# Products of zeros on TensorE inside each norm, between the transposes of two blocks of tokens and behind them

## The chip, the cores and the metric

The kernel runs on one core of one Trainium2 chip. The metric is the device time of one execution in microseconds (us), as the median of the runs. TensorE has two clock levels, 1.2 and 2.4 GHz; the profile shows the granted level of each stretch as a share (0.50 or 1.00). Engine names in the rows are the profile's: PE is TensorE's matmul, PEld its weight load, DVE VectorE, ACT ScalarE, POOL GpSimd, SP the queue that issues transfers.

## What the reference computes

Two blocks in a row on 256 tokens of 1024 features, all in float32. The first has two layers; in each, tokens `x` and a context `ctx` of 256 tokens are normalised, projected, run through a convolution and a two-way recurrent scan, projected back, normalised again and passed through a gated feed-forward layer (FFN):

```
ux = modulate(rmsnorm(x, norm1_g[l]), sh1, sc1) @ w_in[l]
...
x = x + gt1 * (mix_x @ w_out[l])
x = x + gt2 * swiglu(modulate(rmsnorm(x, norm2_g[l]), sh2, sc2), ffn_wg[l], ffn_wu[l], ffn_wd[l])
```

The context takes the same path in layer 0; in layer 1 only its scan states are needed. The second block has two layers of FFN, mixer and FFN, with a layer norm behind each:

```
x = layer_norm(ALPHA * x + 0.5 * swiglu_2(x, ffn1_w13[l], ffn1_w2[l]), ln_g[l, 0], ln_b[l, 0])
x = layer_norm(ALPHA * x + m, ln_g[l, 1], ln_b[l, 1])
x = layer_norm(ALPHA * x + 0.5 * swiglu_2(x, ffn2_w13[l], ffn2_w2[l]), ln_g[l, 2], ln_b[l, 2])
```

## The kernel before

All large products are made of three products of fp32r halves (high by high, high by low, low by high). Weights stream from HBM in tiles of 512 KB (`raw`); `wsplit` makes the high half on ACT (`wh`) and the low half on DVE (`wl`). Tokens stand in two blocks of 128, `b` = 0 and 1, one token to a partition, where the norms are computed: per block the statistics, then the scaled block `yb[b]`. The products need features on partitions, so `feature_major` transposes both blocks: eight transposes of 128x128 for each block on PE into four PSUM tiles (`acc`), where each tile holds two of the eight feature groups `f`, both blocks of each. Then ACT, DVE and POOL evacuate in an order written out by hand (`EVAC`): for each `f` a scaling out of PSUM ("e", over both blocks at once, lines 452 to 458), the high half ("h", line 460) and the low half ("l", line 462). The products that follow walk over `f`. In several norms (`PINS`, and all of the second part of the program) the splits of the third to sixth weight tile behind a norm are held back until the evacuation has ended (`hold`).

The path with `acc=True` is taken eleven times; the text numbers these norms in order of time. The first five are in the first part of the program (`self.tags is TAGS1`): the first before the FFN of the context, the second before its projection of layer 1, the third before the FFN of `x`, the fourth before the projection of `x` in layer 1, the fifth before its FFN. In the second part (`TAGS2`) the sixth is the closing norm of the first block, and the seventh to eleventh are the layer norms (`ln`) in front of mixers (seventh, tenth) and FFNs (eighth, ninth, eleventh). The first six are RMS norms: `rms_blocks` takes the sums of squares of both blocks first (line 416), then both square roots (384), then scales both blocks (423, 425). A layer norm does one block after the other (`ln_norm`, 406).

The order of instructions on each engine is set by a scheduler that runs when the program is built; `issue_after` fixes that one instruction stands behind another on its engine. PE executes its products in that order. `gate_row` builds a gate with eight small products (`tDb`, DVE line 519, PE, ACT copy 521) for the step behind the FFN. PSUM tiles `ps` and `pb` have two buffers each.

A tile of zeros, `zer`, is there already: in `chain` one product of zeros clears a bank ahead of products that accumulate into it.

Of the kernel before, what the change touches and what calls it, by code (L numbers as in the profile page):

```python
# [14 lines left out]
P = 128  # L15
D = 1024
NF = 8
T = 256
# [13 lines left out]
NFIRST = 2  # L32

NLATE = 3

NLAST = 2, 4

# [221 lines left out]
class Prog:  # L259
# [168 lines left out]
    def feature_major(self, yb, scale, bias, perm=False, new=None, acc=True):  # L428

        nc = self.nc  # L430
        new = new or self.S
        hs = [new([P, 4, T], F32R) for _ in range(2)]
        ls = [new([P, 4, T], F32R) for _ in range(2)]

        pt = [self.pacc(i) if acc else self.ps(lane="b") for i in range(4)]
        pt = [t.rearrange("p (j b t) -> p j b t", j=2, b=2) for t in pt]
        for f, b in [(f, b) for b in range(2) for f in range(NF)] if acc else [(f, b) for f in range(NF) for b in range(2)]:
            nc.tensor.transpose(pt[f // 2][:, f % 2, b, :], yb[b][:, f * P : f * P + P], self.cst("ident"))  # L438

        last, ts = {}, {}  # L440
        for e, op, f in (EVAC if acc else EVAC1):
            hi, lo = hs[f // 4][:, f % 4, :], ls[f // 4][:, f % 4, :]
            eng = {"A": nc.scalar, "D": nc.vector, "P": nc.gpsimd}[e]
            with self.tc.issue_after(last[e].ins) if e in last and acc else contextlib.nullcontext():
                if op == "e":
                    ts[f] = t = self.T1([P, T])
                    src, dst = pt[f // 2][:, f % 2].rearrange("p b t -> p (b t)"), t
                    if perm:
                        src = src.rearrange("p (r c) -> p r c", c=64)
                        dst = t.rearrange("p (c r) -> p r c", r=4)  # L450
                    if e == "A" and bias is None:
                        i = nc.scalar.activation(dst, src, AF.Copy, scale=scale(f))
                    elif e == "A":
                        i = nc.scalar.activation(dst, src, AF.Identity, bias=bias(f), scale=scale(f))
                    elif bias is None:
                        i = nc.vector.tensor_scalar(dst, src, scale(f), None, ALU.mult)
                    else:
                        i = nc.vector.tensor_scalar(dst, src, scale(f), bias(f), ALU.mult, ALU.add)
                elif op == "h":
                    i = nc.scalar.copy(hi, ts[f])  # L460
                else:
                    i = eng.tensor_sub(lo, ts[f], hi.bitcast(F32))
            last[e] = i
        la, ld = last["A"], last["D"]
        self.npin += 1
        if self.tags is TAGS2 or self.npin in PINS:
            self.hold, self.since = (la.ins, ld.ins), 0
        return [(hs[f // 4][:, f % 4, :], ls[f // 4][:, f % 4, :]) for f in range(NF)]

    def pacc(self, i):  # L470
        return self.t(self.pa, [P, 512], f"acc{i // 2}{i % 2}")
# [603 lines left out]
    def chain(self, g, AR, GR, KB, uv, r0, Q, pct, st, emit, yall, ends, banks=None):  # L1075

        nc = self.nc
        hd = [(p, d, h) for p in range(2) for d in range(2) for h in range(2)]
        AR, GR, KB = (x[2 * g : 2 * g + 2] for x in (AR, GR, KB))

        def ps(n):
            shape = (P, 2, 2, CH)
            return self.ps(shape) if banks is None else self.t(self.pa if n < 2 else self.pp, shape, banks[n])

        for i in range(4):
            jj = (i, 7 - i)
            sl = slice(i, 8 - i, 7 - 2 * i)
            if st is not None:
                p1 = ps(0)
                for p, d, h in hd:  # L1090
                    q = slice(h * 64, h * 64 + 64)
                    self.mm(p1[q, p, d, :], AR[p][q, d, jj[d] % 4, 0, :], st[q, p, d, :])
                rs = self.T1([P, 2, 2, CH])
                nc.vector.tensor_add(rs, p1, r0[:, :, sl, :])
                rr = lambda q, p, d: rs[q, p, d, :]
            else:
                rr = lambda q, p, d: r0[q, p, jj[d], :]
            pu = [ps(1), ps(0)]
            for p, d, h in hd:
                q = slice(h * 64, h * 64 + 64)  # L1100
                self.mm(pu[h][64:128, p, d, :], Q[d][q, (2 * g + p) * 4 + jj[d] % 4, :], rr(q, p, d))
            nc.scalar.mul(uv[0][64:128, :, sl, :], pu[0][64:128], -1.0)
            nc.vector.tensor_scalar(uv[1][64:128, :, sl, :], pu[1][64:128], -1.0, None, ALU.mult)
            pn = ps(1)
            for p, d, h in hd:
                q = slice(h * 64, h * 64 + 64)
                self.mm(pn[q, p, d, :], KB[p][:, jj[d], q], uv[h][:, p, jj[d], :])
            sn = self.t(self.pool, [P, 2, 2, CH], "st", bufs=5)
            pcb = pct[:, 2 * g : 2 * g + 2, sl].unsqueeze(3).broadcast_to([P, 2, 2, CH])
            if st is not None:  # L1110
                nc.vector.tensor_add(sn, pn, st)
                nc.vector.tensor_mul(sn, sn, pcb)
            else:
                nc.vector.tensor_mul(sn, pn, pcb)
            if emit:
                py = ps(2)
                kd = lambda d: d if i < 2 else 1 - d
                half = lambda h: slice(h * 64, h * 64 + 64)
                if st is not None:

                    self.mm(py.rearrange("p a b t -> p (a b t)"), self.zer[:, 0:P], self.zer, True, False)
                    for p, d, h in hd:
                        q = half(h)
                        self.mm(py[q, p, kd(d), :], st[q, p, d, :], AR[p][q, d, jj[d] % 4, 1, :], False, False)
                for n, (p, d, h) in enumerate(hd):
                    self.mm(py[half(h), p, kd(d), :], uv[h][:, p, jj[d], :], GR[p][:, h, jj[d], :], st is None,
                            st is None or n >= 6)
                lo = min(i, 3 - i)
                ysl = yall[:, 2 * g : 2 * g + 2, :].rearrange("p a (c t) -> p a c t", t=CH)[:, :, lo : 4 - lo : 3 - 2 * lo, :]
                if i < 2:  # L1130
                    nc.scalar.copy(ysl, py)
                else:
                    nc.vector.tensor_add(ysl, py, ysl)
            st = sn
            if i == 3:
                ends.append(st)
            yield
# [28 lines left out]
    def affine(self, x, y, g, b=None):  # L1166


        nc = self.nc
        for _ in range(NLATE):  # L1170
            yield
# [404 lines left out]
TAGS2 = {  # L1576
    ("S", "r"): ("S", 18), ("T1", "r"): ("T1", 10), ("T2", "r"): ("T2", 10), ("tD", "r"): ("tD", 2),
    ("tiny", "r"): ("tn", 8),
}


def body(tc, ap):
    k = Prog(tc, ap)
    with (
# [7 lines left out]
        mk = lambda pool, shape, name, dt=F32: pool.tile(shape, dt, name=name)  # L1592
# [2 lines left out]
        k.const = mk(pc, [P, NCONST], "const")  # L1595
        k.lb = [mk(pc, [P, 4], f"lb{l}") for l in range(2)]
        k.omlb = [mk(pc, [P, 4], f"omlb{l}") for l in range(2)]
        with (
            tc.tile_pool(name="p1", bufs=1) as p1,
            tc.tile_pool(name="pd", bufs=1, space=bass.MemoryType.DRAM) as pd,  # L1600
        ):
            k.pool, k.tags = p1, TAGS1
            k.csil = mk(p1, [P, 8, 32], "csil")
            k.zer = mk(p1, [1, T], "zer", mybir.dt.bfloat16)
            k.mod = [mk(p1, [P, 6, 8, 2], f"mod{l}") for l in range(2)]
            k.omka = [mk(p1, [P, 4], f"omka{l}") for l in range(2)]
            k.keep = [mk(pd, [P, D], f"keep{b}") for b in range(2)]
            k.first()
# [30 lines left out]
```

## Time and profile before

| | us |
|---|---|
| median of 3 runs | 2779.92 |
| lowest and highest run | 2776.57, 2785.88 |
| the profiled execution, its own time | 2783.58 |
| span of its instructions | 2781.8 |
| PE busy in the span | 2632.1 (95%) |
| ACT, DVE, POOL busy | 1327.3, 1716.4, 670.2 |

The profiled execution lies 3.66 above the median, and 1.8 of its time lies outside the span. A busy PE is not PE at its peak, since the ends of products are modelled and overlap. Times in rows count from the start of the span. `a<-b` is the tile written and the tiles read; `L438` is line 438; a bracket at a row's end gives the idle time ahead of it on its engine and what ended it.

### The profile page before, as it was taken

The page shows a single profiled execution, that of the slowest core. Times are in us where ns is not written, and L with a number is a line of the kernel's source. Part 1 is how long each engine was busy: PE and PEld are TensorE (multiplying, and loading weights), DVE is VectorE, ACT ScalarE, POOL GpSimd, SP SyncE. Part 2 cuts the span into 40 slices and gives each one's busy share as a digit, 9 for nine tenths or more (in the row PEclk, how much of TensorE's full clock was granted, in tenths as well). Part 3 has the DMA queues.
Part 4 walks back from the last instruction along what each step waited for, and adds up shares of the span by engine and source line. Part 5 has one row for each costly group of instructions (what it writes and reads, how often), then busy time and mean ns, then how long its engine had stood idle before and what let it go on. Part 6 is the DMA issues. An engine that isn't in the chain of part 4 may idle for free.

```text
span 2781.8 us, 53780 instructions
## 1 busy us (share of the span) xinstructions
PE 2632.1 (95%) x22398; PEld 2291.3 (82%) x22398; DVE 1716.4 (62%) x2703; ACT 1327.3 (48%) x2015; POOL 670.2 (24%) x669
## 2 busy tenths in 40 slices
PE   7889989999889998899899899999999999999998
PEld 4866867888678896866699899889899898889897
DVE  3885778645577555984555655666655655755655
ACT  5523654434565346433544544654544544644543
POOL 0388999920130001384200000010000000100000
PEclk9989989999899999979899999999999999999999
DMA  7345425334323354234355555524555555425653
GB/s 250 109 145 175 147 84 180 132 130 157 117 77 116 136 182 144 95 137 153 117 187 185 194 183 188 193 87 156 182 187 185 182 188 174 166 83 182 205 184 120
DMA packets 118768, 430.71 MB, mean 155 GB/s; under 512 B 13174, under 2 KB 13686, under 8 KB 118524
## 3 DMA queue, kind: packets, MB, share of 16 engines
q1 hardware_dynamic: 118524, 427.28, 45.2%
q8 instruction: 175, 2.87, 0.4%
q14 instruction: 69, 0.57, 0.1%
HBM read 425.13 MB, written 2.10 MB: 154 GB/s over the span
## 4 chain that ended last, share of the span: by engine, by line
PE 78%; DVE 11%; ACT 4%; POOL 3%; issue 2%; DMA 2%; SPq 0%; ACTq 0%; DVEq 0%; POOLq 0%
PE pb L333 33%; PE acc L333 25%; PE ps L333 19%; DVE wl L342 3%; DVE T1c L726 1%; POOL tap L732 1%; DVE S L964 1%; DVE T L962 1%; DMA raw<-in_ada 1%; DVE x L621 1%; ACT wh L341 1%; POOL x L733 1%; PE acc L438 1%; DMA raw<-in_wr 0%; DVE T2b L620 0%
## 5 line engine op out<-in xcount | busy, mean ns | idle before, releaser
L342 DVE TENSOR_TENSOR wl<-raw,wh 128x1024 fp32r<-128x1024 f32 (+1 forms) x654 | 811.9, 1245 | 622.2 <-ACT wh L341 391.7
L341 ACT CAST wh<-raw 128x1024 fp32r<-128x1024 f32 (+1 forms) x654 | 681.9, 1046 | 892.3 <-PE pb L333 345.8
L333 PE MATMUL pb<-xf,wh 128*128 128x256 f32 (+1 forms) x2560 | 486.4, 289 | 12.6 <-ACT T1b L585 4.1
L333 PE MATMUL pb<-S,wh 128*128 128x256 f32 x2560 | 492.0, 289 | 4.8 <-DVE S L631 1.8
L333 PEld LDWEIGHTS pb<-xf,wh 128*128 128x128 f32 (+1 forms) x2560 | 409.8, 194 | 26.7 <-DVE T1b L588 6.6
L333 PEld LDWEIGHTS pb<-S,wh 128*128 128x128 f32 x2560 | 408.5, 192 | 22.4 <-issue 11.8
L333 PE MATMUL ps<-S,wh 128*128 128x256 f32 x2048 | 390.4, 287 | 0.6 <-ACT S L460 0.5
L333 PE MATMUL pb<-xf,wl 128*128 128x256 f32 (+1 forms) x1280 | 371.2, 291 | 8.7 <-DVE wl L342 8.7
L365 POOL TENSOR_TENSOR wl<-raw,wh 128x1024 fp32r<-128x1024 f32 x22 | 54.9, 2504 | 1340.4 <-ACT wh L364 826.9
L333 PE MATMUL pb<-S,wl 128*128 128x256 f32 x1280 | 367.4, 287 | 2.0 <-DVE wl L342 2.0
L333 PEld LDWEIGHTS ps<-S,wh 128*128 128x128 f32 x2048 | 326.8, 192 | 9.0 <-issue 3.4
L333 PE MATMUL ps<-S,wl 128*128 128x256 f32 x1024 | 293.4, 286 | 0.6 <-DVE wl L342 0.6
L333 PEld LDWEIGHTS pb<-xf,wl 128*128 128x128 f32 (+1 forms) x1280 | 248.1, 194 | 16.7 <-DVE wl L342 11.5
L333 PEld LDWEIGHTS pb<-S,wl 128*128 128x128 f32 x1280 | 245.4, 192 | 6.6 <-issue 3.0
L333 PE MATMUL acc<-wh,T 128*128 128x512 f32 x704 | 206.3, 393 | 0.0
L333 PEld LDWEIGHTS ps<-S,wl 128*128 128x128 f32 x1024 | 196.7, 192 | 2.8 <-issue 1.4
L333 PE MATMUL acc<-wh,T1b 128*128 128x512 f32 x528 | 157.5, 396 | 3.5 <-ACT T1b L341 3.5
L732 POOL TENSOR_SCALAR tap<-z,cols 128x255 f32<-128x255 f32 (+14 forms) x120 | 149.2, 1252 | 0.0
L333 PEld LDWEIGHTS acc<-wh,T 128*128 128x128 f32 x704 | 126.9, 189 | 23.6
L732 POOL TENSOR_SCALAR tap<-x,cols 128x246 f32<-128x246 f32 (+6 forms) x104 | 111.4, 1079 | 46.1 <-DVE x L671 46.0
L733 POOL TENSOR_TENSOR x<-x,tap 128x247 f32<-128x247 f32 (+8 forms) x132 | 106.8, 809 | 34.4 <-ACT tap L730 28.0
L733 POOL TENSOR_TENSOR z<-z,tap 128x255 f32<-128x255 f32 (+14 forms) x120 | 112.8, 940 | 3.9
(445 smaller groups left out, 3968.7 us busy)
## 6 DMA issues: line engine op xcount, KB each, us to landing
raw<-in_fu SPq DMA_DIRECT2D x132, 512.0 KB, 3.2
raw<-in_ada SPq DMA_DIRECT2D x96, 512.0 KB, 4.3
raw<-in_pu SPq DMA_DIRECT2D x88, 512.0 KB, 4.2
raw<-in_qu SPq DMA_DIRECT2D x88, 512.0 KB, 3.7
raw<-in_fd SPq DMA_DIRECT2D x66, 512.0 KB, 3.2
raw<-in_wr SPq DMA_DIRECT2D x51, 512.0 KB, 3.6
raw<-in_pd SPq DMA_DIRECT2D x44, 512.0 KB, 4.1
raw<-in_qd SPq DMA_DIRECT2D x44, 512.0 KB, 3.8
```

Source lines behind the costliest of these rows:

```text
L333: return self.nc.tensor.matmul(out, lhsT, rhs, start=start, stop=stop, **kw)
L341: self.nc.scalar.copy(hi, src)
L342: self.nc.vector.tensor_sub(lo, src, hi.bitcast(F32))
L365: self.nc.gpsimd.tensor_sub(lo, r, hi.bitcast(F32))
L438: nc.tensor.transpose(pt[f // 2][:, f % 2, b, :], yb[b][:, f * P : f * P + P], self.cst("ident"))
L621: nc.vector.tensor_add(x[b][:, s], x[b][:, s], t)
L726: nc.vector.scalar_tensor_tensor(av[:, d], z[:, f, s], w(j), av[:, d], ALU.mult, ALU.add)
L732: nc.gpsimd.tensor_scalar(t[:, d], z[:, f, s], w(j), None, ALU.mult)
L733: nc.gpsimd.tensor_add(zc[f][:, d], zc[f][:, d], t[:, d])
L962: nc.vector.tensor_mul(tv, tj[:, k + 1 : 32, k : k + 1].broadcast_to([P, m, k + 1]), X[:, k : k + 1, 0 : k + 1].broadcast_to([P, m, k + 1]))
L964: nc.vector.tensor_sub(X[:, k + 1 : 32, 0 : k + 1], X[:, k + 1 : 32, 0 : k + 1], tv)
```

## The change

`feature_major` with `acc=True` chains the transposes: all eight of block 0, then `NZERO` products of zeros (128x128 by 128x256, bfloat16), all eight of block 1, then `NZEND` = 6 products of zeros. `NZERO` is 32 in the first part of the program and 14 in the second. Each such group writes a `ps` or `pb` tile that nobody reads. The tile `zer` grows from one partition to 128 and lives through the whole program; the one product in `chain` reads its first partition, as before.

```diff
+NZERO, NZEND = (32, 14), 6
...
+        last = None
         for f, b in [(f, b) for b in range(2) for f in range(NF)] if acc else [(f, b) for f in range(NF) for b in range(2)]:
-            nc.tensor.transpose(pt[f // 2][:, f % 2, b, :], yb[b][:, f * P : f * P + P], self.cst("ident"))
+            with self.tc.issue_after(last.ins) if last else contextlib.nullcontext():
+                i = nc.tensor.transpose(pt[f // 2][:, f % 2, b, :], yb[b][:, f * P : f * P + P], self.cst("ident"))
+            if acc and f == NF - 1:
+                last = self.zeros(i, (NZERO[self.tags is TAGS2], NZEND)[b])
...
+    def zeros(self, after, n):
+
+        pz = self.ps()
+        for _ in range(n):
+            with self.tc.issue_after(after.ins):
+                after = self.mm(pz[:, 0:T], self.zer[:, 0:P], self.zer)
+        return after
...
-                    self.mm(py.rearrange("p a b t -> p (a b t)"), self.zer[:, 0:P], self.zer, True, False)
+                    self.mm(py.rearrange("p a b t -> p (a b t)"), self.zer[0:1, 0:P], self.zer[0:1, 0:T], True, False)
...
+        k.zer = mk(pc, [P, T], "zer", mybir.dt.bfloat16)
...
-            k.zer = mk(p1, [1, T], "zer", mybir.dt.bfloat16)
```

PE's order around the fifth norm, before the change (`Sb_15174` is block 0, `Sb_15175` block 1, `x2` two transposes):

```order
L333 MATMUL acc_2600_15017<-wh_15134,xf_14950 128x512
L438 MATMUL acc_2643_15202<-const,Sb_15174 128x128 x2
L438 MATMUL acc_2644_15203<-const,Sb_15174 128x128 x2
L438 MATMUL acc_2643_15202<-const,Sb_15175 128x128 x2
L438 MATMUL acc_2644_15203<-const,Sb_15175 128x128 x2
L438 MATMUL acc_2645_15204<-const,Sb_15174 128x128 x2
L438 MATMUL acc_2646_15205<-const,Sb_15174 128x128 x2
L438 MATMUL acc_2645_15204<-const,Sb_15175 128x128 x2
L438 MATMUL acc_2646_15205<-const,Sb_15175 128x128 x2
L333 MATMUL pb_15299<-xf_15198,wh_15289 128x256
```

The same place now (lines are three to fifteen higher; `Sb_15334` is block 0, `Sb_15335` block 1; the pair of rows with `zer` stands 32 times at the first "..." and six times at the second):

```order
L336 MATMUL acc_2608_15177<-wh_15294,xf_15110 128x512
L443 MATMUL acc_2651_15362<-const,Sb_15334 128x128 x2
L443 MATMUL acc_2654_15365<-const,Sb_15334 128x128 x2
L336 LDWEIGHTS zer
L336 MATMUL pb_15374<-zer 128x256
...
L443 MATMUL acc_2651_15362<-const,Sb_15335 128x128 x2
L443 MATMUL acc_2654_15365<-const,Sb_15335 128x128 x2
L336 MATMUL pb_15415<-zer 128x256
...
L336 MATMUL pb_15455<-tDb_15456,const 128x128
L336 MATMUL pb_15469<-tDb_15470,const 128x128
L336 MATMUL pb_15499<-xf_15358,wh_15489 128x256
```

Before, four feature groups of each block came first and the rest behind; now the first transpose of block 1 stands behind all of block 0 and 32 products of zeros. Five products of the gate row (`tDb`), which stood ahead of the norm, now stand between the norm and the first product of the FFN. The same is so in the first and third norm; on DVE the eight `tDb` operations stand among the operations of the evacuation there.

PE's order around the seventh norm, a layer norm, before:

```order
L438 MATMUL acc_3292_19220<-const,S_19198 128x128 x2
L438 MATMUL acc_3295_19223<-const,S_19198 128x128 x2
L438 MATMUL acc_3292_19220<-const,S_19213 128x128 x2
L438 MATMUL acc_3295_19223<-const,S_19213 128x128 x2
L333 MATMUL ps_19279<-S_19216,wh_19282 128x256
```

And now, where the pair with `zer` stands 14 times and then six times:

```order
L443 MATMUL acc_3304_19442<-const,S_19420 128x128 x2
L443 MATMUL acc_3307_19445<-const,S_19420 128x128 x2
L336 LDWEIGHTS zer
L336 MATMUL ps_19454<-zer 128x256
...
L443 MATMUL acc_3304_19442<-const,S_19435 128x128 x2
L443 MATMUL acc_3307_19445<-const,S_19435 128x128 x2
L336 MATMUL pb_19477<-zer 128x256
...
L336 MATMUL ps_19523<-S_19438,wh_19526 128x256
```

Here only the zeros are new: block 0 stood ahead of block 1 before too.

## Rows read from the trace of the kernel before

**Rows 1.** The page: chain that ended last, by engine.

```profile
PE 78%; DVE 11%; ACT 4%; POOL 3%; issue 2%; DMA 2%; SPq 0%; ACTq 0%; DVEq 0%; POOLq 0%
```

**Rows 2.** Timeline of ACT, PE and DVE at the fifth norm: start, length.

```profile
1358.16 1.95 ACT L423 ACTIVATE Sb<-x,tnb 128x512 f32<-128x512 f32 x3
1358.93 3.67 PE L438 MATMUL acc<-const,Sb 128*128 128x128 f32 x16 [8.54 <-ACT Sb L423]
1360.51 0.56 ACT L454 ACTIVATE T1b<-acc,mod 128x256 f32<-128x256 f32 x1 [0.41 <-PE acc L438]
1362.51 0.79 PE L333 MATMUL pb<-xf,wh 128*128 128x256 f32 x2
1369.43 2.36 DVE L342 TENSOR_TENSOR wl<-raw,wh 128x1024 fp32r<-128x1024 f32 x2 [2.34 <-PE pb L333]
```

**Rows 3.** Windows at the fifth norm: busy by engine, granted clock, DMA.

```profile
1361.40:1364.60 3.20, 3.20 (x16) 2.90 (x15) 2.29 (x7) 3.17 (x9) 0.00 (x0) 0.50 0.00 0
1364.80:1368.20 3.40, 3.40 (x30) 3.40 (x30) 1.58 (x4) 2.40 (x5) 1.48 (x2) 1.00 0.00 0
```

**Rows 4.** Fourth norm: timeline of PE and ACT, and one window.

```profile
1072.61 3.67 PE L438 MATMUL acc<-const,S 128*128 128x128 f32 x16 [7.04 <-ACT S L423]
1074.19 0.82 ACT L454 ACTIVATE T<-acc,mod 128x256 f32<-128x256 f32 x1 [0.41 <-PE acc L438]
...
1074.70:1077.90 3.20, 3.20 (x17) 3.18 (x16) 3.01 (x7) 3.14 (x7) 0.09 (x1) 0.50 0.88 329
```

**Rows 5.** Sixth norm: timeline of PE and ACT.

```profile
1564.48 3.68 PE L438 MATMUL acc<-const,x 128*128 128x128 f32 x16 [7.04 <-ACT x L423]
...
1566.11 0.47 ACT L452 ACTIVATE T<-acc,cols 128x256 f32<-128x256 f32 x1 [0.46 <-ACT x L423]
```

**Rows 6.** First, second and third norm: timeline of PE and DVE.

```profile
400.00 0.53 PE L333 MATMUL ps<-S,S 64*32 64x32 f32 x19 [4.16 <-DVE S L850]
...
703.46 0.58 PE L333 MATMUL pb<-S,wh 128*128 128x256 f32 x1 [1.85 <-DVE S L462]
...
825.93 1.04 PE L438 MATMUL acc<-const,Sb 128*128 128x128 f32 x8
...
826.57 0.55 DVE L458 TENSOR_SCALAR T1b<-acc,mod 128x256 f32<-128x256 f32 x1 [0.17 <-PE acc L438]
```

**Rows 7.** Products of the one-partition tile of zeros: shortest, median, longest in ns.

```profile
L333 PE MATMUL ps<-zer x22: 264/278/391, 227.8 to 1295.3; 1*128 1x256 bf16 x22
```

**Rows 8.** Seventh norm: timeline of PE.

```profile
1755.86 1.38 PE L438 MATMUL acc<-const,S 128*128 128x128 f32 x8
1758.88 1.11 PE L438 MATMUL acc<-const,S 128*128 128x128 f32 x8 [1.64 <-DVE S L406]
1760.47 1.04 PE L333 MATMUL ps<-S,wh 128*128 128x256 f32 x2 [0.48 <-ACT S L460]
```

**Rows 9.** Windows behind the eighth, ninth and eleventh norm (L333 alone): PE, PEld, granted clock, DMA.

```profile
1974.70:1978.10 3.40, 3.40 (x27) 3.11 (x27) 1.00 0.61 236
2166.90:2170.20 3.30, 1.59 (x7) 1.59 (x8) 0.50 0.98 391
...
2580.00:2583.20 3.20, 2.15 (x10) 2.15 (x11) 0.50 1.02 323
```

**Rows 10.** Timeline: first transposes, and fifth FFN activation, of the eighth, ninth, eleventh norm.

```profile
1969.86 1.39 PE L438 MATMUL acc<-const,S 128*128 128x128 f32 x8
...
2014.60 0.38 ACT L585 ACTIVATE T<-ps 128x256 f32<-128x256 f32 x1
...
2163.76 1.38 PE L438 MATMUL acc<-const,S 128*128 128x128 f32 x8
...
2208.82 0.37 ACT L585 ACTIVATE T<-pb 128x256 f32<-128x256 f32 x1
...
2576.50 1.38 PE L438 MATMUL acc<-const,S 128*128 128x128 f32 x8
...
2621.31 0.38 ACT L585 ACTIVATE T<-pb 128x256 f32<-128x256 f32 x1
```

## The prediction, made before the changed kernel ran

> **What bounds the kernel now.** I began with the chain that ended last: PE is 78% of it, DVE 11% [rows 1]. So the end of the program moves with PE's work and with the waits between PE's stretches, and a norm is such a place: PE stops, two blocks are normalised, transposed and evacuated, and only then the next products start. So I next read the timeline around each of the eleven norms, then the granted clock there. The reader is to see two kinds of norm.
>
> In the RMS norms both blocks are ready nearly together. At the fifth, ACT's scaling of three half blocks takes 1.95 us from 1358.16, PE has been idle for 8.54 us, and all sixteen transposes run without a hole, 3.67 us, which is 0.23 each at the half clock (0.50); the evacuation starts at 1360.51, after the sixth transpose, because the order before alternated the blocks [rows 2, 3]. The fourth and sixth look alike: 7.04 us idle, then 3.67 and 3.68 us for sixteen [rows 4, 5]. In the layer norms block 1 comes later: after block 0's eight transposes PE waits 1.64 us for DVE, and 0.48 us behind block 1's [rows 8].
>
> **What the change costs and gives.** *One product of zeros.* It has the shape of the FFN's products. Those ran at 3.40 us for 30, 0.113 each, at the full clock, and I use this; at the half clock I use the transposes' 0.23 [rows 2, 3]. Zeros of another shape (one partition) are in the trace with a modelled length of 0.278, which is the bound from above if nothing of it overlapped [rows 7].
>
> *Fifth norm.* Block 0's eight end at 1358.93 + 8 x 0.23 = 1360.8. The clock stood at 0.50 until 1364.6 with PE busy on real products [rows 3], and I keep that time: (1364.7 - 1360.8) / 0.23 = 17 products of zeros at half clock, the other 15 x 0.113 = 1.7, end at 1366.4. The first "e" needs feature 0 of both blocks, so add one transpose of block 1 (0.11) and the 0.20 that lie before the change between six transposes (1358.93 + 6 x 0.23 = 1360.31) and ACT's start: 1366.7 against 1360.51, 6.2 late. Some of it comes back, since what follows runs at the full clock: the first 48 FFN products took 1362.51 to 1369.43, where DVE's next weight split waits for PE, 6.9 us against 48 x 0.113 = 5.4; I write that as 1.5 back. Net 4.7. Then the gate row: its eight operations on DVE, which lay in the idle time before, now stand among the evacuation's, and PE walks all of one weight tile before the other, so that some 18 products (18 x 0.113 = 2.0) are left when the last feature is ready instead of few. The eight on DVE are about as long (8 x 0.25, an estimate from halves of the evacuation's 0.55 [rows 6]). They overlap; I take 2, bounds 0 and 4. Sum for this norm +6.7.
>
> *Fourth norm.* Block 0 ends at 1074.45; the clock was 0.50 to 1077.9 [rows 4]: 15 products at 0.23, 17 at 0.113, end 1079.8; evacuation at 1080.1 instead of 1074.19, +5.9. Back: the products from 1076.3 (the end of the transposes) to 1077.9 ran at half clock, 0.8. Net +5.1; no gate row here.
>
> *Sixth norm.* 14 products, all at the half clock that its transposes show: 1564.48 + 1.84 + 14 x 0.23 = 1569.5, evacuation at 1569.8 against 1566.11, +3.7, with 0.8 back as in the fourth: +2.9 [rows 5].
>
> *Third norm.* Block 1's transposes began at 825.93 and ran at 0.13 each, the full clock. With zeros ahead of them: 825.9 + 32 x 0.113 = 829.5, evacuation from 829.8 against 826.57 [rows 6]: +3.2, and 2 for the gate row as in the fifth: +5.2.
>
> *First and second norm* are mixed with the scan of `x`, so the zeros lie partly in waits. In the first PE waits 4.16 us for DVE in the middle of the transposes, which covers most of the zeros; but products of the FFN that now run between two groups of the scan move behind the second group. In the second, PE waits 1.85 us for the evacuation itself, which the zeros make later, while the clock may stay up [rows 6]. I take +2 (bounds -2 and +6) and 0 (bounds -4 and +5).
>
> *Seventh to eleventh norm.* 14 x 0.113 = 1.58 fits into the hole of 1.64 plus the last transpose's tail; six more, 0.68, fill the 0.48 hole and the tail ahead of it [rows 8]. So they delay nothing; what they can give is the clock. The trace has its own test of that. Behind the ninth and eleventh norm the clock falls to 0.50 for some 3.3 us, behind the eighth it does not [rows 9], and all three are followed by the same FFN. From the first transpose to the fifth activation of the FFN: 2014.60 - 1969.86 = 44.74 with the full clock, 45.06 and 44.81 with the fall [rows 10]. The fall costs 0.32 and 0.07, not the 1.65 that half of 3.3 would be, because the first products wait for the evacuation and then for weight splits, which lose nothing. Mean 0.2, four norms with a fall: -0.8 in all. Bounds: all halves lost, 4 x 1.65 = -6.6; and with a pitch of 0.278, 14 x 0.278 = 3.9 against 1.75 of hole, five times +2.1.
>
> *The rest.* The tile of zeros on 128 partitions is one memset at the program's start, under the first transfers; the product in `chain` is the same. Other rows of the first part change places because the scheduler sees longer norms; I put no sum on it and +-5 us into the range.
>
> Sum: 2 + 0 + 5.2 + 5.1 + 6.7 + 2.9 - 0.8 = +21.1. The profiled execution took 2783.58, so it would take 2804.7; it lies 3.66 above the median, and by the median 2779.92 + 21.1 = 2801.
>
> **The rivals.** *The early norms pay it back.* The first three norms have the longest waits; if the zeros lie wholly in them and the clock stays up for the products after, each gives 3 back instead of costing: -9 + 5.1 + 6.7 + 2.9 - 0.8 = +4.9, some 2785. The 4.16 us wait speaks for it, PE's FFN behind these norms, where each product of zeros is PE's time, against it. 0.17.
>
> *The clock decides: faster.* If PE's pace is the bound behind each norm and the zeros fall into waits, every norm gives the half of its stretch at 0.50: 11 x 1.65 = 18, some 2762. It decides if block 1 of an RMS norm is ready more than 5 us behind block 0, which no row of the fourth to sixth shows. The Trainium skill, page "TensorE: Matmul & The Clock Gate", section "Why this matters for your kernels", advises to keep TensorE busy without gaps so that it keeps its full clock; by it the change does right at all eleven places. The trace agrees that the clock falls in these gaps, but the eighth norm against the ninth and eleventh [rows 9, 10] shows that little of it reaches the end. 0.09.
>
> *Zeros at 0.278.* Layer norms +2.1 each, 15 x 0.165 = 2.5 more in the fourth and fifth and 32 x 0.165 = 5.3 in the third: 10.5 + 5.0 + 5.3 on top of the sum, 2822. The modelled length of an FFN product is near 0.28 too at a pitch of 0.113, which speaks against it. 0.05.
>
> *Zeros don't lift the clock.* Then the change doesn't do what it says: all 32 at 0.23 (7.4 against 5.6) and more at half clock behind, some 2 more at each of the third to fifth norm, and the layer norms' holes are overrun where the clock falls: 14 x 0.23 = 3.2 against 1.75, 1.5 each at four: 2801 + 6 + 6 = 2813. 0.07.
>
> **How the numbers follow.** My forecast, the zeros of the RMS norms delay block 1, has 0.62, with a range of its own from 2790 to 2814. A measurement of this kernel can tell about 0.3%, 8.3 us, from no change: slower is above 2788.3, faster below 2771.6. The forecast, the pitch and the clock that is not lifted are slower: 0.62 + 0.05 + 0.07 = 0.74; early payback is the same, 0.17; the clock is faster, 0.09. The range reaches down to 2781, past the most of the payback case, and up to 2814.
>
> **What would show it.** Right: at the fourth and fifth norm a gap of some 5.5 us between block 0's and block 1's transposes, filled with zeros of 0.23 and then 0.113, and the first evacuation 6 us later behind block 0 than before; at the layer norms block 1's first transpose still 3.0 us behind block 0's, clock 1.00 behind it, and the fifth FFN activation at 44.7 to 44.8 us in all three; gate row copies inside the evacuation of the fifth. Wrong: if the zeros are shorter than 0.113, if the clock rises much earlier inside them, if the weights' splits and not the evacuation start the products after the fourth to sixth norm, or if the moved rows of the first part gain or lose more than 5 us.

## The result and the profile after

The changed kernel took 2822.37 us (median of 4 runs, 2817.22 to 2826.88) against 2782.9 for the kernel before in the same session: a ratio of 1.0142, 95% interval 1.0121 to 1.0164, or 39.5 us more. The profiled execution took 2826.88 us, with a span of 2825.1 against 2781.8.

**The fifth norm.** Timeline of PE, where [rows 2] had one row of sixteen transposes:

```profile
1391.68 1.97 PE L443 MATMUL acc<-const,Sb 128*128 128x128 f32 x8 [8.54 <-ACT Sb L426]
1393.44 4.84 PE L336 MATMUL pb<-zer 128*128 128x256 bf16 x32
1398.12 1.04 PE L443 MATMUL acc<-const,Sb 128*128 128x128 f32 x8
...
1402.55 0.70 PE L336 MATMUL pb<-tDb,const 128*128 128x128 f32 x2 [1.14 <-DVE tDb L534]
1402.91 0.77 PE L336 MATMUL pb<-xf,wh 128*128 128x256 f32 x2
```

ACT at the same place, its first evacuation:

```profile
1398.54 0.56 ACT L461 ACTIVATE T1b<-acc,mod 128x256 f32<-128x256 f32 x1 [5.69 <-PE acc L443]
```

Windows (as in [rows 3]) early and late inside these zeros, products alone:

```profile
1393.50:1395.50 2.00, 2.00 (x10) 1.44 (x10) 0.50 0.00 0
1396.00:1398.00 2.00, 2.00 (x20) 1.80 (x19) 1.00 0.00 0
```

Ten zeros took 2 us at the half clock and twenty at the full one, 0.2 and 0.1 each. The 32 hold block 1 back by 4.7 us in which PE runs nothing else. ACT starts 6.86 us behind block 0's first transpose, not 1.58 as in [rows 2]. Then come five products of the gate row (`tDb`; each is two records in a row's count), the last of them 1.14 us late for want of DVE, and the FFN starts at 1402.91: 4.37 us behind the first evacuation, where it was 2.00 [rows 2].

**The fourth and the sixth norm**, timeline of PE:

```profile
1094.39 1.97 PE L443 MATMUL acc<-const,S 128*128 128x128 f32 x8 [7.05 <-ACT S L426]
1096.15 5.00 PE L336 MATMUL ps<-zer 128*128 128x256 bf16 x32
1100.99 1.04 PE L443 MATMUL acc<-const,S 128*128 128x128 f32 x8
...
1606.17 1.97 PE L443 MATMUL acc<-const,x 128*128 128x128 f32 x8 [6.96 <-ACT x L426]
1607.93 3.14 PE L336 MATMUL pb<-zer 128*128 128x256 bf16 x14
1610.91 1.04 PE L443 MATMUL acc<-const,x 128*128 128x128 f32 x8
```

They answer to [rows 4, 5]: block 1 begins 6.60 and 4.74 us behind block 0. Before, four transposes of 0.23 stood ahead of it, 0.9 us.

**The first norm**, timeline of PE, and below it DVE:

```profile
390.86 1.76 PE L443 MATMUL acc<-const,Sb 128*128 128x128 f32 x8
392.46 3.66 PE L336 MATMUL pb<-zer 128*128 128x256 bf16 x32
395.95 1.04 PE L443 MATMUL acc<-const,Sb 128*128 128x128 f32 x8
...
406.03 0.61 PE L336 MATMUL pb<-tDb,const 128*128 128x128 f32 x4
413.64 1.48 PE L336 MATMUL pb<-tDb,const 128*128 128x128 f32 x4 [7.00 <-DVE tDb L534]
...
421.00 1.06 PE L336 MATMUL pb<-tDb,const 128*128 128x128 f32 x4
421.71 0.77 PE L336 MATMUL pb<-xf,wh 128*128 128x256 f32 x2
```

```profile
410.88 1.51 DVE L889 TENSOR_TENSOR S<-S,T 128x512 f32<-128x512 f32 x1
412.31 1.96 DVE L534 TENSOR_SCALAR tDb<-const,mod 128x128 f32<-128x128 f32 x2
```

The kernel before at the same place, timeline of PE:

```profile
389.67 0.49 PE L333 MATMUL pb<-tDb,const 128*128 128x128 f32 x2
393.02 2.82 PE L438 MATMUL acc<-const,Sb 128*128 128x128 f32 x12 [2.87 <-ACT Sb L423]
...
404.88 0.90 PE L333 MATMUL pb<-xf,wh 128*128 128x256 f32 x3
```

The zeros themselves are short here, 0.11 each at the full clock. The idle time that stands out is behind them: 7.00 us in which PE waits for a `tDb` of the gate row, which DVE makes only behind operations of the evacuation and of the scan. Before, the gate row was done ahead of the norm. The FFN's first product now starts 30.85 us behind block 0's first transpose, where it was 11.86.

**The layer norms**, timeline of PE at the ninth, and windows of products alone behind the eighth, ninth and eleventh (compare [rows 8, 9]):

```profile
2210.92 1.38 PE L443 MATMUL acc<-const,S 128*128 128x128 f32 x8
2212.14 1.69 PE L336 MATMUL ps<-zer 128*128 128x256 bf16 x14
2213.95 1.11 PE L443 MATMUL acc<-const,S 128*128 128x128 f32 x8
```

```profile
2022.20:2025.60 3.40, 3.40 (x27) 3.12 (x26) 1.00 0.59 235
2214.10:2217.40 3.30, 2.50 (x18) 2.17 (x19) 1.00 0.69 236
2622.30:2625.50 3.20, 2.73 (x20) 2.45 (x21) 1.00 0.93 294
```

The first transposes of the eighth and eleventh norm and the fifth FFN activations of all three, to hold against [rows 10]:

```profile
2017.33 1.39 PE L443 MATMUL acc<-const,S 128*128 128x128 f32 x8
...
2062.05 0.38 ACT L600 ACTIVATE T<-ps 128x256 f32<-128x256 f32 x1
...
2255.74 0.37 ACT L600 ACTIVATE T<-pb 128x256 f32<-128x256 f32 x1
...
2618.79 1.38 PE L443 MATMUL acc<-const,S 128*128 128x128 f32 x8
...
2663.35 0.38 ACT L600 ACTIVATE T<-pb 128x256 f32<-128x256 f32 x1
```

Zeros fill the hole, block 1 still starts 3.03 us behind block 0, the clock does not fall. With block 0 first at 2017.33, 2210.92 and 2618.79 the activations stand 44.72, 44.82 and 44.56 us behind, against 44.74, 45.06 and 44.81: where the clock fell before, at the ninth and eleventh, the full clock is worth about 0.25 us a norm.

**Where the time went, by stretch.** From the first transpose of one norm to that of the next, us more than before, in the profiled execution of the changed kernel and of those below (read off the timelines as above; the first column counts from the span's start, the last from the seventh norm to the span's end):

| kernel | to 1 | 1-2 | 2-3 | 3-4 | 4-5 | 5-6 | 6-7 | 7-end |
|---|---|---|---|---|---|---|---|---|
| changed kernel | -2.2 | +16.6 | -4.2 | +11.6 | +11.0 | +8.9 | +2.6 | -1.0 |
| ln_only | +8.1 | +2.2 | -2.2 | +1.4 | +0.5 | +2.8 | +0.1 | +1.4 |
| n1to3 | +2.2 | +16.8 | -3.5 | +10.9 | -1.0 | 0.0 | -0.1 | -1.9 |
| n4to6 | -0.3 | 0.0 | -0.1 | 0.0 | +16.8 | +6.6 | +2.9 | -0.5 |
| inpt | +0.7 | +0.7 | -0.4 | +6.8 | +15.3 | +5.3 | +2.8 | -1.8 |
| end0 | -6.8 | +15.8 | -2.3 | +12.0 | +11.6 | +7.9 | +3.1 | -1.8 |
| tile1 | +1.4 | +6.5 | -6.5 | +6.5 | -1.4 | +3.9 | +0.2 | +4.3 |
| inpt16 | +4.5 | +0.8 | -5.0 | +6.1 | +20.6 | +2.3 | +2.8 | -1.4 |
| chain | +2.4 | -2.6 | +3.0 | +2.7 | +3.2 | +0.2 | +0.2 | -2.0 |
| rot | -0.6 | 0.0 | -0.1 | 0.0 | +5.5 | -2.0 | -0.1 | -1.1 |
| ahead | +3.8 | -0.3 | -1.7 | +1.5 | +4.4 | +2.6 | -1.1 | -1.1 |
| ahead56 | +4.1 | -0.5 | -2.4 | +1.5 | -1.7 | +1.6 | -1.3 | -1.0 |

Every row of the table is one execution, held against one of the kernel before. ln_only keeps the rows of before up to the seventh norm and still differs by up to 2.8 in a stretch and 8.1 at the start; d4, below, keeps them up to the fourth and differs by 4.1 in the stretch 3-4. Single stretches are therefore read to some 4 us, and totals by the medians.

### The profile page after: what moved, and what is told of

It is laid out like the page before. It is cut to its first block, busy times and chain, and to the rows that moved or that the text cites. A ratio compares the mean times of both kernels' runs of the same rounds, so it can differ in the third digit from the quotient of the medians.

```text
span 2825.1 us, 54405 instructions
## 1 busy us (share of the span) xinstructions
PE 2665.1 (94%) x22708; PEld 2322.0 (82%) x22708; DVE 1715.7 (61%) x2703; ACT 1325.0 (47%) x2014; POOL 664.7 (24%) x669
## 5 line engine op out<-in xcount | busy, mean ns | idle before, releaser
L336 PEld LDWEIGHTS ps<-S,wh 128*128 128x128 f32 x2048 | 325.0, 191 | 10.9 <-issue 3.7
L336 PEld LDWEIGHTS acc<-wh,T1b 128*128 128x128 f32 x528 | 95.8, 192 | 23.2 <-ACT T1b L344 4.4
L336 PE MATMUL acc<-wl,T 128*128 128x512 f32 x352 | 113.2, 395 | 0.0
```

What stands on the lines that cost most here:

```text
L336: return self.nc.tensor.matmul(out, lhsT, rhs, start=start, stop=stop, **kw)
```

## The experiments

Diffs are against the changed kernel unless another is named. `self.npin - 1` is the norm's number.

**Which norms.** Three kernels with zeros and held order at some norms only.

```diff
+NORMS = 7, 8, 9, 10, 11
...
-            if acc and f == NF - 1:
+            if acc and f == NF - 1 and self.npin - 1 in NORMS:
```

and with `NORMS = 1, 2, 3` and `NORMS = 4, 5, 6`.

> Zeros and the held order of blocks only at norms 7 to 11, the first six as before. Theory (all of the loss lies in the first part; at the layer norms the 14 fit into the hole of 1.64 us): -1.0 us against before, worked out from the changed kernel's shifts between norm 7 and the end (+3.2 - 0.3 - 0.3 - 4.6 + 1.0), so the same within what can be told; norm 9 and 11 reach the 48th product behind the first transpose after 10.7 us instead of 11.3 and 11.2. Rival (zeros hold the clock up and PE's pace bounds the layer norms): -6.6 us, 1.65 at each of four. Rival (zeros overrun the hole): +2 or more.

Measured: 2786.87 against 2787.39, ratio 0.9996 [0.9979, 1.0013]. The same.

> Zeros and the held order only at norms 1 to 3. Theory (the loss of the first three norms is one of moved rows near them, as the trace of the changed kernel has it between its start and norm 4: -2.2 + 16.6 - 4.2 + 11.6): +22 us against before. Rival (the prediction's sum for these three norms was right and the rest came from something that the later norms do): 2 + 0 + 5.2 = +7 us. Rival (they pay back): 0 or below.

Measured: 2806.72 against 2787.39, ratio 1.0070 [1.0043, 1.0097], +19.5 us.

> Zeros and the held order only at norms 4 to 6. Theory (block 1 waits for the zeros and the products behind it are late, 11.0 + 8.9 + 2.6 by the trace of the changed kernel): +22 us against before, the end of block 1's transposes 6 to 7 us behind block 0's at norms 4 and 5. Prediction's sum for these three: 5.1 + 6.7 + 2.9 = +14.7; that is left if the further loss behind norm 4 (a longer stretch at half clock at 1245 to 1290 us) was not the zeros' doing. Rival (they pay back): 0 or below.

Measured: 2808.08 against 2787.39, ratio 1.0074 [1.0049, 1.0098], +20.6 us.

The three add up: 1.0070, 1.0074 and 0.9996 make 1.0140, the changed kernel's 1.0142. The layer norms give and take nothing that can be told (the interval reaches from -5.9 to +3.6 us), and the loss lies half at the first three norms, for which the prediction had 7.2, and half at the next three, for which it had 14.7.

**The tile of the zeros.** In inpt the zeros between the blocks go into PSUM columns that block 1's transposes fill next, so they take no tile of their own; the six behind block 1 are gone.

```diff
-                last = self.zeros(i, (NZERO[self.tags is TAGS2], NZEND)[b])
+                last = self.zeros(i, NZERO[self.tags is TAGS2], pt[3][:, :, 1, :]) if b == 0 else i
...
-    def zeros(self, after, n):
+    def zeros(self, after, n, pz):
...
-        pz = self.ps()
...
-                after = self.mm(pz[:, 0:T], self.zer[:, 0:P], self.zer)
+                after = self.mm(pz, self.zer[:, 0:P], self.zer.rearrange("p (a b) -> p a b", a=2))
```

> The zeros between the blocks (32, 14) written into the columns of the transposes' own bank that block 1 fills afterwards, so that they take no PSUM tile from the pool that the gate row and the scan use; the six behind block 1 are left out. The scan's and FFN's products behind norm 1 then stand in the order of before. Theory (tile: the zeros' tile pushes the gate row and the rows of the scan behind them, the excess over the prediction at norms 1, 3 and 5): 1 to 2 gives +2 to +5 instead of +16.6, 3 to 4 some +6 instead of +11.6, in all +22 to +27 us against before. Rival (delay alone: block 1 late by 4 to 6 us and what follows from that): +36 to +40, the six zeros behind block 1 being worth some 1 us a norm at most. Rival (the schedule of the first part is a matter of chance): anywhere between 0 and +40, with the loss in other stretches than in the changed kernel.

Measured: 2806.03 against 2787.39, ratio 1.0057 [1.0034, 1.0081], +15.9 us by the ratio: under half of the loss, and less than the +22 to +27 expected. PE at the first norm of inpt:

```profile
390.33 0.49 PE L336 MATMUL pb<-tDb,const 128*128 128x128 f32 x2
393.68 1.97 PE L443 MATMUL acc<-const,Sb 128*128 128x128 f32 x8 [2.87 <-ACT Sb L426]
395.45 5.60 PE L336 MATMUL acc<-zer 128*128 128x256 bf16 x32
...
403.93 0.36 PE L336 MATMUL pb<-xf,wh 128*128 128x256 f32 x1
```

The gate row is done ahead of the norm again, and the FFN starts 10.25 us behind block 0's first transpose. The zeros are longer here (5.60 us against 3.66), and yet the stretch 1-2 costs 0.7 us instead of 16.6. Which tile it was, the 32's or that of the six, the next run tells.

```diff
-            if acc and f == NF - 1:
-                last = self.zeros(i, (NZERO[self.tags is TAGS2], NZEND)[b])
+            if acc and f == NF - 1 and b == 0:
+                last = self.zeros(i, NZERO[self.tags is TAGS2])
...
-        pz = self.ps()
+        pz, self.psn = self.ps(), self.psn + 1
```

> The changed kernel without the six products of zeros behind block 1 and without their tile; the 32 (14) between the blocks stay in a tile of their own. Beside the run with the zeros in the transposes' own bank it differs by that one tile alone. Theory A (the tile of the 32 keeps the gate row's tile back): norm 1 to 2 some +15 as in the changed kernel, DVE's gate row waited for some 7 us by PE, in all +34 to +40 us. Theory B (the six behind block 1 and their tile are what puts the gate row behind the scan group): norm 1 to 2 +1 to +5, in all +18 to +27.

Measured: 2823.74 against 2785.06, ratio 1.0134 [1.0108, 1.0161]. Nearly the whole loss, so the six behind block 1 are not it. PE at the first norm of end0:

```profile
391.74 0.61 PE L336 MATMUL pb<-tDb,const 128*128 128x128 f32 x4
...
410.23 1.23 PE L336 MATMUL pb<-tDb,const 128*128 128x128 f32 x4 [5.33 <-DVE tDb L534]
411.11 0.77 PE L336 MATMUL pb<-xf,wh 128*128 128x256 f32 x2
```

The FFN starts 24.84 us behind block 0's first transpose (386.27). Between inpt and end0 the zeros' own tile makes 1.0134 - 1.0057 = 0.0077, about 21 us, give or take 10 by the two intervals; end0 also moves the turn of the PSUM tiles on, as the changed kernel does, which by rot, below, makes some 3 us in all, not clear of the noise, and nothing in the stretch 1-2. The code says how: the pool has two buffers of `pb`, dealt out in program order; `modulated` asks for the zeros' tile, and only then `ffn_add` for the gate row's two. So the gate row's later tile waits until the zeros, and with them block 0's transposes, are done. Does the tile cost as much when almost no zeros hold it? In tile1 one product of zeros is left at each of the first five norms (the expectation says six; the sixth is in the second part and gets none).

```diff
-NZERO, NZEND = (32, 14), 6
+NZERO, NZEND = (1, 0), 0
...
-            if acc and f == NF - 1:
+            if acc and f == NF - 1 and b == 0 and self.tags is not TAGS2:
...
-        pz = self.ps()
+        pz, self.psn = self.ps(), self.psn - 1
```

> At each of the first six norms one product of zeros behind block 0 in place of 32 (14), none behind block 1, none at norms 7 to 11: it keeps a tile of the pool until block 0's transposes are done, but takes 0.23 us at most, so what it costs is the tile. Theory (the gate row's products need that tile's place in turn, so the gate row, which nothing else binds to the norm, is put behind block 0's transposes, at norm 1 behind the scan's group on DVE too): norm 1 to 2 +10 to +16 us, 3 to 4 +3 to +6, 5 to 6 +2.5 to +3.5, 2 to 3 and 6 to 7 within 1, 4 to 5 some +3 (its rows are those of the run with the order alone); in all +18 to +25 us against before. Rival (the tile hurts only together with the 3.7 to 5 us that 32 products of zeros hold it): norm 1 to 2 below +5 and in all +3 to +10.

Measured: 2792.02 against 2786.22, ratio 1.0023 [1.0007, 1.0038], +6.4 us. Too low for my theory. PE at the first norm of tile1:

```profile
396.04 0.27 PE L336 MATMUL pb<-zer 128*128 128x256 bf16 x1
396.15 0.61 PE L336 MATMUL pb<-tDb,const 128*128 128x128 f32 x4
...
402.21 0.49 PE L336 MATMUL pb<-tDb,const 128*128 128x128 f32 x2 [3.56 <-DVE tDb L534]
...
415.85 0.80 PE L336 MATMUL pb<-tDb,const 128*128 128x128 f32 x2 [4.35 <-DVE tDb L534]
416.29 0.77 PE L336 MATMUL pb<-xf,wh 128*128 128x256 f32 x2
```

The gate row is behind block 0's transposes as foretold, the waits for `tDb` are there, and the FFN starts 21.85 us behind the first transpose (394.44), but the stretch 1-2 loses 6.5 us only and 2-3 gives 6.5 back. So a displaced gate row with hardly any zeros costs some 6 us in all; by these single executions the rest needs the tile and the delay of 32 zeros together, more than the sum of the two (0.7 and 6.5 against 16 in the stretch 1-2).

**The size of the delay**, with `NZERO, NZEND = (16, 14), 6` in inpt.

> As the run with the zeros in the transposes' own bank, but 16 between the blocks instead of 32 at norms 1 to 5 (norm 6 and the layer norms keep 14). Theory (the delay is the time that the zeros take, which at the half clock is 16 x 0.23 = 3.7 us for the first 16 and the rest at 0.113): norm 5 to 6 +3.3 to +4.2 instead of +5.3, 3 to 4 (at the full clock) half of +6.8, and the first 130 us behind norm 4 +3 instead of +4; norm 6 to 7 +2.8 as before. What the scan behind norm 4 does with its other order is not forecast by either theory: 4 to 5 anywhere between +3 and +14. In all +10 to +20. Rival (the count does not matter, it is the hold on block 1's order): 5 to 6 stays at +5.3, 3 to 4 at +6.8.

Measured: 2814.7 against 2786.22, ratio 1.0106 [1.0078, 1.0134]: half the zeros at norms 1 to 5 and a larger loss, +29.5 us where +10 to +20 was expected. The stretch 5-6 (+2.3 for +5.3) went with the zeros' time, 3-4 hardly (+6.1 for +6.8), and 4-5 went the other way: +20.6, the largest of all runs. So something there is not the delay.

**The scan behind the fourth norm.** Three kernels alter rows without any zeros between the blocks. First the held order alone:

```diff
-NZERO, NZEND = (32, 14), 6
+NZERO, NZEND = (0, 0), 0
...
-        pz = self.ps()
+        pz = self.ps() if n else None
```

> The order of blocks held (block 0's eight transposes, then block 1's) at all eleven norms, with no product of zeros and no tile for them. Theory (loss = zeros that delay block 1, plus rows that move because the zeros take a tile and lengthen the norm): the first evacuation of norms 4 to 6 waits for two more transposes, 0.23 each, so +0.5 at each of them, the scan behind norm 4 changes 259 rows and may cost up to 5; in all 0 to +7 us against before. Rival (the order of the blocks itself is the loss, through the weights' walk behind it): +15 or more, with 2 to 5 at each norm 3 to 6.

Measured: 2789.78 against 2785.06, ratio 1.0006 [0.9990, 1.0021]. The order of the blocks costs nothing that can be told.

Then the kernel before with the turn of the PSUM tiles moved on:

```diff
         pt = [t.rearrange("p (j b t) -> p j b t", j=2, b=2) for t in pt]
+        self.psn += 2 * acc
```

> Before with one thing changed: at each of the eleven norms the counter that deals out the PSUM tiles in turn is moved on by two, as the two tiles of zeros do, without any zeros. It moves rows only in the scan of x in layer 1 (645 rows of PE between norms 4 and 5). Theory A (between norms 4 and 5 the loss over the 5 us of the delayed block, 6 to 12 us in three kernels, is the scan's other interleaving and no work of the zeros): 4 to 5 takes +5 to +12 us, with a longer stretch at half clock at 150 to 200 us behind norm 4, and the rest +0. Rival B (the scan is late because the norm is late): 0 within 2 us.

Measured: 2786.92 against 2785.06, ratio 1.0012 [0.9999, 1.0024]. The stretch 4-5 is +5.5, all of it in the scan, though the longer half clock that I forecast there is absent.

Then zeros in PE's idle time ahead of the norms:

```diff
-NZERO, NZEND = (32, 14), 6
+NAHEAD = 56
+NORMS = 4, 5, 6
...
-        return self.nc.tensor.matmul(out, lhsT, rhs, start=start, stop=stop, **kw)
+        self.lastmm = self.nc.tensor.matmul(out, lhsT, rhs, start=start, stop=stop, **kw)
+        return self.lastmm
...
-        last = None
+        last = self.zeros(self.lastmm, NAHEAD) if acc and self.npin - 1 in NORMS else None
...
-            if acc and f == NF - 1:
-                last = self.zeros(i, (NZERO[self.tags is TAGS2], NZEND)[b])
...
-        pz = self.ps()
+        pz, self.psn = self.ps(), self.psn - 1
```

> No zeros between or behind the blocks; instead 56 products of zeros right behind the last product ahead of norms 4, 5 and 6, in PE's idle time of 7.0 to 8.5 us there (56 x 0.113 = 6.3 us), order of blocks as before. Theory (the zeros of the change hurt only because they stand where block 1 waits for them; in true idle time they delay nothing and give the clock): the sixteen transposes take 1.8 us instead of 3.67 and the products behind them start at the full clock, 0.7 to 2 us earlier at each of three norms: -2 to -6 us, with up to +-5 from the 266 rows that change places in the scan behind norm 4. Rival (the clock there is worth nothing, what follows waits for ACT and DVE): 0. Rival (zeros cost wherever they stand): +5 or more.

Measured: 2789.47 against 2785.06, ratio 1.0018 [1.0006, 1.0030]: some 5 us slower, against my theory. PE at the fourth norm of ahead:

```profile
1068.72 6.29 PE L337 MATMUL ps<-zer 128*128 128x256 bf16 x56
1075.93 1.97 PE L445 MATMUL acc<-const,S 128*128 128x128 f32 x16 [0.92 <-ACT S L428]
```

The local part came true: sixteen transposes in 1.97 us instead of 3.67 [rows 4], and the products some 110 to 130 us on were 2.5 us early. The scan then lost 6.9. With norm 4 left out (`NORMS = 5, 6`):

> 56 products of zeros ahead of norms 5 and 6 alone, in PE's idle time, so that norm 4 and nearly all of the scan behind it keep their rows (66 of PE move). Theory (in the run with them at norms 4, 5 and 6 the first 130 us behind norm 4 were 2.3 us earlier and the scan then lost 7 of its own by its other order): norm 4 to 5 within 1.5, 5 to 6 and 6 to 7 -0.7 to -1.1 each, in all -2 us, not to be told from before by the median. Rival (the gain is lost whatever follows): 5 to 6 and 6 to 7 at 0 or above.

Measured: 2783.71 against 2786.22, ratio 0.9993 [0.9978, 1.0008]. No gain that can be told. The scan's loss is gone (4-5 at -1.7), norm 6 gave its 1.3, norm 5 did not (+1.6). PE at the fifth norm of ahead56:

```profile
1351.18 6.29 PE L337 MATMUL pb<-zer 128*128 128x256 bf16 x56
1357.31 0.61 PE L337 MATMUL pb<-tDb,const 128*128 128x128 f32 x4
1359.90 3.42 PE L445 MATMUL acc<-const,Sb 128*128 128x128 f32 x16 [1.98 <-ACT Sb L428]
1363.11 1.50 PE L337 MATMUL pb<-tDb,const 128*128 128x128 f32 x6
```

It is the gate row again, now behind the zeros' tile and around the transposes.

To part the scan's order from the delay, four kernels, each executed once, have zeros at norm 4 alone, in the transposes' own bank. The diff is that of inpt and, with 48, 24, 8 and 4 for the count,

```diff
-NZERO, NZEND = (32, 14), 6
+NZERO, NZEND = (48, 14), 6
...
+            if acc and f == NF - 1 and self.npin - 1 == 4:
```

> 48 products of zeros between the blocks of norm 4 alone, in the transposes' own bank; the delay is the longest (32 gave 5.1 to 5.3 us between the first transposes of the blocks more than before and +3.9 us some 100 us behind the norm; 16 more at 0.113 make +5.7), but only 74 rows of PE change places in the scan behind the norm. Theory O (what the scan loses over the delay is its other order): norm 4 to 5 takes +5 to +8 us, with PE idle 3 to 5 us and 30 to 40 us at half clock at 130 us and more behind the norm, as before. Theory D (the scan loses because the norm is late): +16 us or more, with 7 us or more idle and 54 us or more at half clock there.

> 24 products of zeros at norm 4 alone, in the transposes' own bank: a shorter delay (some +3.3 us at 100 us behind the norm), but 297 rows of PE change places. Theory O (order): +3.3 and 3 to 17 more, so more than the run with 48; Theory D (delay): less than the run with 48, in proportion some +12.

> 8 products of zeros at norm 4 alone, in the transposes' own bank: delay some +1.3 us; 263 rows change places, and the order is within 68 rows that of the run with the order of blocks alone, which took +3.2 between norms 4 and 5. Theory O (order): +3 to +6. Theory D (delay): in proportion to 32, some +4; this run tells the two apart least and gives the curve its lower end.

> 4 products of zeros at norm 4 alone, in the transposes' own bank: delay some +0.7 us; only 50 rows change places. Theory O (order): within -1 and +2. Theory D (delay): some +2.

Measured: 2795.13, 2794.55, 2790.14 and 2791.09 against 2793.02 for one execution of the kernel before beside them, so the whole time shows none of what follows. In the stretch 4-5: +9.9 (between the two theories, nearer to O), +11.1, +3.8 and +1.5. Next to the others, with the delay taken as the median by which PE's products 110 to 130 us behind the norm are later than before, and the scan's loss as the rest of the stretch. Rows moved are those of PE that stand elsewhere in the program between norms 4 and 5 than before or write another tile; the zeros themselves are counted in, so that d48 has 26 without its 48:

| kernel | PE rows moved | delay | rest | whole stretch |
|---|---|---|---|---|
| d48 | 74 | +7.2 | +2.7 | +9.9 |
| d4 | 50 | +0.1 | +1.4 | +1.5 |
| d8 | 263 | +1.9 | +1.9 | +3.8 |
| chain | 259 | +1.7 | +1.5 | +3.2 |
| changed kernel | 616 | +5.3 | +5.7 | +11.0 |
| rot | 645 | -0.2 | +5.7 | +5.5 |
| d24 | 297 | +4.3 | +6.8 | +11.1 |
| ahead | 266 | -2.5 | +6.9 | +4.4 |
| inpt | 348 | +3.1 | +12.2 | +15.3 |
| n4to6 | 759 | +3.9 | +12.9 | +16.8 |
| inpt16 | 220 | +4.6 | +16.0 | +20.6 |

The longest delay, with 26 moved rows beside its zeros, loses 2.7 us beside it, no more than the spread of a stretch; a norm that is early (ahead) or on time (rot) loses as much as one that is 4 to 5 us late. By these executions the scan's loss is not a consequence of the late norm. It comes with a moved order, but the number of moved rows does not tell its size, and a moved order need not cost: n1to3 and tile1 have 250 and 261 rows moved there by the same count, and their stretch 4-5 came out at -1.0 and -1.4. The scan's windows, from 130 us behind norm 4 to 50 us ahead of norm 5, busy time of PE, PEld, DVE, ACT, POOL, then granted clock; before:

```profile
1202.60:1308.90 106.30, 103.26 (x1407) 72.15 (x1406) 66.83 (x154) 36.24 (x65) 67.85 (x80) 0.83 0.46 160
```

the changed kernel:

```profile
1224.40:1341.70 117.30, 110.02 (x1431) 77.17 (x1432) 69.24 (x154) 33.87 (x62) 72.02 (x86) 0.75 0.44 156
```

d48:

```profile
1206.50:1322.70 116.20, 108.67 (x1451) 75.26 (x1452) 73.98 (x169) 36.68 (x66) 74.69 (x88) 0.84 0.46 163
```

inpt16:

```profile
1209.00:1335.90 126.90, 109.75 (x1415) 76.58 (x1412) 68.92 (x158) 35.12 (x64) 70.56 (x84) 0.77 0.42 142
```

PE's idle time in them is 106.30 - 103.26 = 3.0, then 7.3, 7.5 and 17.2 us, and the mean clock 0.83, 0.75, 0.84 and 0.77. The changed kernel and inpt16 lose in both ways, in idle time and at the half clock. d48 keeps the clock of before but has the idle time that the theory of the delay foretold, and rot, with no delay, has 7.3 us idle at 0.86 in its window (1202.0 to 1313.8): idle time here does not tell the two theories apart.

## Why the prediction was right in direction and wrong in size

The sign was right, and at the fourth to sixth norm so was the mechanism of the forecast: the zeros hold block 1 back, and what follows waits. At the first norm the mechanism was another. By its own steps:

- *Fifth norm, +6.7.* Stretch 5-6: +8.9. First evacuation 5.3 us late where 6.2 was written, since 32 zeros took 4.84 us and not 5.6. inpt, with the gate row ahead, has +5.3 beside the 4.7 for the delay; the rest, 3.6, goes by this difference to the gate row, where 2 stood (bounds 0 and 4).
- *Fourth norm, +5.1.* The delay is +5.3 at 110 to 130 us; the same 32 zeros gave +3.9 in n4to6 and +3.1 in inpt, so the step was right to some 2 us. The scan's +5.7 behind it had no term.
- *Sixth norm, +2.9.* Stretch 6-7: +2.6; +2.8 and +2.9 in inpt and n4to6.
- *Seventh to eleventh, -0.8.* -1.0 in the trace, but +1.4 in that of ln_only, so the agreement is luck; the run with these alone cannot be told from before. Zeros of 1.69 us fit into the hole, as written, and the 0.25 at the ninth and eleventh are near the 0.2 written.
- *Third norm, 3.2 + 2 = +5.2.* Stretch 3-4: +11.6. In the changed kernel the 32 zeros took 1.51 + 2.46 us, not 3.6, with eight transposes of the scan between them. inpt, with the gate row ahead, has +6.8, which leaves 4.8 for the gate row, not 2. The 6.8 is not all delay: half the zeros left +6.1 (inpt16), and none +2.7 (chain).
- *First norm, +2 (bounds -2 and +6).* This is the step that failed. It counted zeros in waits and the FFN's products behind the second scan group. By inpt that much was right: +0.7. It put the gate row at nothing, which it counted at the fifth and third norm and which moves here too. Here DVE has the scan to do as well, the `tDb` are waited for up to 7.00 us, the FFN starts 30.85 us behind the first transpose instead of 11.86, and the stretch 1-2 took +16.6.
- *Second norm, 0.* Stretch 2-3: -4.2; -0.4 in inpt, -6.5 in tile1. That it gives back part of what the first norm lost is not shown: inpt16 has -5.0 behind +0.8.
- *Moved rows of the first part, 0 +- 5.* The second failure. The scan behind norm 4 lost 5.7 in the changed kernel and up to 16 in its relatives, by one execution each.

The excess over the sum, 39.5 - 21.1 = 18.4 us by the medians and 43.3 - 21.1 = 22.2 in the profiled executions, is thus 14.6 in the stretch 1-2, less 4.2 in 2-3, 6.4 in 3-4, 5.9 in 4-5 and 2.2 in 5-6; the start (-2.2) and the last stretches (-0.5) make up the rest of the 22.2. The rival with zeros at 0.278 gave the time measured, 2822, for a reason that the trace refutes: they took 0.11 each at the full clock. The rival "zeros don't lift the clock" fell at the fifth norm, where the granted clock went from 0.50 to 1.00 inside the zeros, and the early payback fell with the +19.5 us of n1to3. The rival "the clock decides" fell too: PE kept its full clock, 1.00, behind all layer norms, and the run with these norms alone gained nothing that can be told. The Trainium skill, page "TensorE: Matmul & The Clock Gate", section "Why this matters for your kernels", advises to keep TensorE busy, without idle gaps between bursts of products, so that its clock stays up. The trace agrees on the clock (1.00 behind these norms), and shows that it is worth 0.25 us at one of them. What stays open is which moved rows of the scan cost how much, and why tile and delay together cost more than each by itself at the first norm: no run held the scan's order fixed, though d48 comes near it.

## What to carry to other kernels

An instruction that does nothing still takes a buffer, and in a pool that deals them out in turn this binds whoever asks next to it. Write such fillers into space that is about to be overwritten anyway, put them where an engine has true idle time, and look at what asks for the same buffers next. Even so none of the placements tried here made the kernel faster. Where a scheduler interleaves long streams, give a local edit a margin for the order that changes 100 us away: here it was as large as the edit.

## What was not expected of the hardware

- A full clock at a norm is worth little when evacuation and weight splits set the pace: 0.25 us at a layer norm for 3.3 us that had been at half. Where it did help, transposes at the full clock (1.97 us for sixteen, not 3.67), an RMS norm gave 1.1 us (stretch 6-7 of ahead) to 2.5 us (the fourth norm of ahead), in one execution each.
- The clock came back late for zeros as for products: all 14 at the sixth norm ran at the half clock, 3.14 us. Zeros that end 0.92 us ahead of the transposes left them the full clock (ahead, fourth norm); in ahead56 at the fifth norm, where two products of the gate row and 1.98 us of idle time lay between, sixteen transposes took 3.42 us.
- The start of the program, up to the first norm, took from 6.8 us less to 8.1 us more than in the execution before, and the 8.1 with the rows of before: a span of 15 us, over a third of what the change cost.
